# Feed-forward chunks 1 to 8 of a decoder layer: gate and up products computed together in eight PSUM banks, with two of eight pairs of K-blocks as seven products of sums

## The chip, the cores and the metric

The kernel runs on one core of a Trainium2 chip. The metric is the device time of one execution in microseconds (us). Of the kernel before there are three timed runs and one profiled execution.

## What is computed

One layer of a decoder trunk for 256 tokens of width 2048, in float32: a token mixer (retention, differential attention and a spatial gating unit, fed by one input projection and followed by an output projection) and a SwiGLU feed-forward of width 5632, each between two RMS norms. The part that matters here is the feed-forward:

```
h = rms_norm(x, pre_ffn_g[l])
f = (jax.nn.silu(h @ w_gate[l]) * (h @ w_up[l])) @ w_down[l]
x = x + rms_norm(f, post_ffn_g[l])
```

`h` is 256 x 2048, `w_gate` and `w_up` are 2048 x 5632, `w_down` is 5632 x 2048.

## The kernel before

Every large product is made of float32 operands that are split in two: `hi` is the operand rounded to the narrower matmul format fp32r (a ScalarE copy), `lo` is what is left (a VectorE subtraction). A product is then three matmuls, hi times hi, lo times hi, and hi times lo. The weights arrive as 512 KB pieces of two K-blocks (2 x 128 rows) by 512 columns; `split_weights` loads a piece into `raw` (4 buffers), writes `hi` (5 buffers) and `lo` (5 buffers). The activations, here `x1_hi` and `x1_lo`, stay in SBUF, transposed, with 256 tokens as two blocks `tb` of 128.

The hidden width of 5632 is walked in 11 chunks of 512 columns. For one chunk `matmul_chunk` runs over the eight weight pieces (16 K-blocks) of `w_gate` and accumulates one PSUM bank for each token block (the pool `acc`, 4 banks), then does the same for `w_up`. So a piece feeds 2 K-blocks x 2 token blocks x 3 = 12 matmuls of 128x512, and a chunk has 16 pieces, or 192 matmuls. `gate_part` reads the gate banks (tanh on ScalarE, then a VectorE operation) into a tile `fa`; `up_part` multiplies the up banks into it, waits one step, and then transposes the result: eight 128x128 transposes on TensorE into two tiles `h_ps` (the pool `tr`, 2 banks), a ScalarE copy to the hi half of the hidden activation and a VectorE subtraction to its lo half (line 582). The steps of `up_part` are taken by `advance()`, which is called after each weight piece.

The down projection already uses another scheme, in `seven_products`. Two token blocks and two K-blocks of the activation, and two K-blocks and two column chunks of the weights, are 2 x 2 blocks each; their product is formed with seven block products of sums instead of eight plain ones. The sums of the weight blocks are formed on VectorE from two raw pieces, the sums of the activation blocks once by `token_sums`. Seven banks collect the seven products over all pairs that use the scheme ("S" pairs); `partial_sums` then combines banks 0, 4, 5 and 6. Plain pairs ("P") add to banks 1, 2, 3 and 7, so that after both kinds each of the four results is one of these banks plus one partial sum. In the down projection one of three pairs is S. This stage uses all 8 banks; the pools are `acc` (4 banks), `tr` (2) and `mx` (2).

Instructions are written in program order; a scheduler then orders them for each engine and gives out the buffers of the pools, and an engine runs its own list strictly in that order. Loads are issued on SP's queue, in order.

Of the kernel before, what the change touches and what calls it, by code (L numbers as in the profile page):

```python
# [8 lines left out]
F32 = mybir.dt.float32  # L9
# [24 lines left out]
def trunk(  # L34
# [521 lines left out]
    h_parts = []  # L556
    for i, n in enumerate((2, 2, 2, 2, 3)):
        part = hpool.tile([P, 2, 4 * n, T], F32R, tag=f"h{i}", name=f"h{i}")
        h_parts += [(part, 4 * j) for j in range(n)]

    def h_chunk(c):
        part, k0 = h_parts[c]
        return part[:, 0, k0:k0 + 4], part[:, 1, k0:k0 + 4]

    def h_of(kb):
        hi, lo = h_chunk(kb // 4)
        return hi[:, kb % 4], lo[:, kb % 4]

    def up_part(c, aa, accs):
        for tb in range(NT):  # L570
            a = aa[tb]
            nc.vector.scalar_tensor_tensor(out=a, in0=a, scalar=hrr[:, tb:tb + 1], in1=accs[tb],
                                           op0=ALU.mult, op1=ALU.mult)
        yield
        for tb in range(NT):
            pt = ps_tr.tile([P, 4, P], F32, tag="tr", name="h_ps")
            for i in range(4):
                nc.tensor.transpose(out=pt[:, i], in_=aa[tb][:, i * P:(i + 1) * P], identity=ident)  # L578
            ts = slice(tb * P, (tb + 1) * P)
            h_hi, h_lo = h_chunk(c)  # L580
            nc.scalar.copy(out=h_hi[:, :, ts], in_=pt)
            nc.vector.tensor_tensor(out=h_lo[:, :, ts], in0=pt, in1=h_hi[:, :, ts].bitcast(F32), op=ALU.subtract)  # L582

    pending.append(up_part(0, aa, up0))
    for c in range(1, NCH):
        accs = matmul_chunk(w_gate[c], KB, 512, x1_of)
        aa = [gate_part(tb, accs[tb]) for tb in range(NT)]
        accs = matmul_chunk(w_up[c], KB, 512, x1_of)
        pending.append(up_part(c, aa, accs))


    actx.close()
    dn = ctx.enter_context(tc.tile_pool(name="dn", bufs=1))
    ss_f = const.tile([P, NT, 4], F32, tag="ss_f", name="ss_f")
    ss_t = const.tile([P, NT], F32, tag="ss_t", name="ss_t")
    ro_f = const.tile([P, NT], F32, tag="ro_f", name="ro_f")
    part_ss = const.tile([P, NT], F32, tag="part_ss", name="part_ss")
# [3 lines left out]
    def token_sums(c):  # L601

        hi, lo = h_chunk(c)
        tmp = dn.tile([P, 2, 1024], F32, tag="wide", name="sums_f")
        a = tmp[:, 0].rearrange("p (q e t) -> p q e t", q=2, e=2)
        f = tmp[:, 1].rearrange("p (q s t) -> p q s t", q=2, s=4)
        nc.vector.tensor_tensor(out=tmp[:, 0].rearrange("p (k t) -> p k t", k=4), in0=hi.bitcast(F32),
# [8 lines left out]
        home = dn.tile([P, 2, 2, 4, P], F32R, tag=f"sums{c}", name=f"sums{c}")  # L616
# [5 lines left out]
        for q in range(2):  # L622
            sums[2 * c + q] = [(home[:, 0, q, j], home[:, 1, q, j]) for j in range(4)]

    def fetch(n, p):
        raw = wraw.tile([P, 2, 512], F32, tag="raw", name="raw")
        nc.sync.dma_start(out=raw, in_=w_down[n][p])
        return raw
# [16 lines left out]
    def seven_products(n0, p):
        ra, rb = fetch(n0, p), fetch(n0 + 1, p)
        h1 = wsplit.tile([P, 2, 512], F32R, tag="hi", name="hi")
        l1 = wsplit.tile([P, 2, 512], F32R, tag="lo", name="lo")
        h22 = dn.tile([P, 512], F32R, tag="h22", name="hi_22")
        l22 = dn.tile([P, 512], F32R, tag="l22", name="lo_22")  # L650
# [4 lines left out]
        for out, in0, in1, op in ((ra[:, 0], ra[:, 0], rb[:, 0], ALU.subtract), (rb[:, 0], rb[:, 1], rb[:, 0], ALU.subtract),  # L655
# [11 lines left out]
        s1n, s2, s3, s4 = sums[p]  # L667
        return [[(0, h_block(2 * p, 0), (h1[:, 0], l1[:, 0])),
                 (1, h_block(2 * p + 1, 0), (h1[:, 1], l1[:, 1])),
# [4 lines left out]
                 (3, h_block(2 * p + 1, 1), (h2[:, 1], l2[:, 1]))]]  # L674

    def bank_tile(i):
        pool, tag = ((ps_tr, "tr"), (ps_acc, "acc"), (ps_acc, "acc"), (ps_acc, "acc"), (ps_tr, "tr"), (ps_mx, "mx"),
                     (ps_mx, "mx"), (ps_acc, "acc"))[i]
        return pool.tile([P, 512], F32, tag=tag, name=f"bank{i}")

    def down_columns(n0, new_fg, seq, extra, finish, tail_pairs, order):
# [4 lines left out]
        banks = {}  # L686
        kinds = [k for k, _ in seq]
        last_s = max(i for i, k in enumerate(kinds) if k == "S")
        left = {}
        for i, (k, _) in enumerate(seq):  # L690
            for b, n in (((1, 2), (2, 2), (3, 2), (7, 2)) if k == "P" else tuple((b, 1) for b in range(7))):
                left[b] = left.get(b, 0) + n
        for b, n in ((1, 2), (2, 2), (3, 2), (7, 2)):
            left[b] += n * len(tail_pairs)
        begun = set()

        def product(b, a, w):
            if b not in banks:
                banks[b] = bank_tile(b)
            left[b] -= 1  # L700
            (a_hi, a_lo), (w_hi, w_lo) = a, w
            nc.tensor.matmul(banks[b], lhsT=a_hi, rhs=w_hi, start=b not in begun, stop=False)  # L702
            nc.tensor.matmul(banks[b], lhsT=a_lo, rhs=w_hi, start=False, stop=False)  # L703
            nc.tensor.matmul(banks[b], lhsT=a_hi, rhs=w_lo, start=False, stop=left[b] == 0)  # L704
            begun.add(b)

        part = {}

        def partial_sums():
            u = dn.tile([P, 512], F32, tag="u", name="u")  # L710
            nc.scalar.copy(out=fg[:, 0, 0:512], in_=banks[0])
            nc.vector.tensor_tensor(out=u, in0=fg[:, 0, 0:512], in1=banks[5], op=ALU.add)
            nc.vector.tensor_tensor(out=fg[:, 0, 512:1024], in0=u, in1=banks[4], op=ALU.add)
            nc.vector.tensor_tensor(out=fg[:, 1, 512:1024], in0=fg[:, 0, 512:1024], in1=banks[6], op=ALU.add)
            nc.vector.tensor_tensor(out=fg[:, 1, 0:512], in0=u, in1=banks[6], op=ALU.add)

        for i, (k, p) in enumerate(seq):
            if i in extra:
                extra[i]()
            for part in (plain_pair(n0, p) if k == "P" else seven_products(n0, p)):  # L720
                for b, a, w in part:
                    product(b, a, w)
            advance()
            if i == last_s:
                fg = new_fg()
                partial_sums()
        parts = [plain_pair(n0, p) for p in tail_pairs]
# [28 lines left out]
    def new_fg(pool, tag):  # L756
# [5 lines left out]
                 {0: lambda: token_sums(2), 5: lambda: token_sums(3), 11: lambda: token_sums(4)}, close_chunk, [20, 21],  # L762
# [126 lines left out]
```

## Time and profile before

| | |
|---|---|
| median of 3 runs | 1139.25 us (1138.71 to 1139.56) |
| profiled execution, its own time | 1139.24 us |
| its span, first to last instruction | 1137.5 us |
| TensorE (PE) busy | 1123.8 us, 99% |
| VectorE (DVE) busy | 707.3 us, 62% |
| ScalarE (ACT) busy | 550.7 us, 48% |
| mean granted TensorE clock | 0.998 |

The busy time of TensorE overlaps itself, because the record of a matmul lasts longer than the distance to the next. What a matmul costs is read from the distance between starts. The feed-forward up to the last hidden chunk runs from about 400 us to 905 us, the down projection from about 894 us to the end.

### The profile page before, as it was taken

The numbers are of one execution on the slowest core, as the hardware profiler recorded it, in microseconds if no ns is written. First come the engines' busy times: TensorE is split into PE (matmuls) and PEld (weight loads), VectorE is DVE, ScalarE is ACT, GpSimd is POOL, SyncE is SP. The second block draws the span as 40 slices with busy tenths as digits, with TensorE's granted clock in tenths as the row PEclk, the third lists the DMA queues.
The fourth block names the chain that finished last, engine by engine and source line by source line (L and its number), as shares of the span: only waits on it lengthen the run. The fifth ranks groups of instructions, "written<-read, shape, count | busy, mean of one in ns | idle before, by whom it ended". The sixth has DMA issues, their size and how long they took to land.

```text
span 1137.5 us, 14030 instructions
## 1 busy us (share of the span) xinstructions
PE 1123.8 (99%) x5246; PEld 945.2 (83%) x5246; DVE 707.3 (62%) x867; ACT 550.7 (48%) x750; POOL 27.3 (2%) x55
## 2 busy tenths in 40 slices
PE   9999999999999999999999999999999999999996
PEld 7888899998888878888888888888888878888885
DVE  6655555656768596555554555555555787877775
ACT  7644455655644464444444444444444444555451
POOL 0000000000200000000000000000000000000000
PEclk9999999999999999999999999999999999999999
DMA  9755455565566446555555555555555366565662
GB/s 360 265 186 189 162 159 181 167 227 185 172 231 210 168 153 231 186 185 193 190 190 188 188 198 185 186 194 190 189 187 189 131 216 222 206 208 197 222 207 90
DMA packets 65013, 221.35 MB, mean 195 GB/s; under 512 B 7344, under 2 KB 9392, under 8 KB 64432
## 3 DMA queue, kind: packets, MB, share of 16 engines
q1 hardware_dynamic: 64656, 220.30, 57.1%
q8 instruction: 41, 0.67, 0.2%
q14 instruction: 28, 0.23, 0.1%
q10 hardware_dynamic: 288, 0.15, 0.1%
HBM read 218.32 MB, written 2.10 MB: 194 GB/s over the span
## 4 chain that ended last, share of the span: by engine, by line
PE 97%; DVE 1%; issue 1%; DMA 0%; ACT 0%; SPq 0%; POOLq 0%; POOL 0%; DVEq 0%; ACTq 0%
PE acc L90 25%; PE acc L88 25%; PE acc L89 25%; PE bank L704 6%; PE bank L703 6%; PE bank L702 6%; PE h_ps L578 1%; DMA raw<-in_w_ret_dram 0%; PE qk_ps L235 0%; PE sc L267 0%; PE x_ps L496 0%; PE yt_ps L191 0%; PE o_ps L244 0%; PE o_ps L243 0%; PE o_ps L242 0%
## 5 line engine op out<-in xcount | busy, mean ns | idle before, releaser
L81 DVE TENSOR_TENSOR lo<-raw,hi 128x1024 fp32r<-128x1024 f32 (+2 forms) x385 | 455.9, 1188 | 367.2 <-ACT hi L79 346.2
L79 ACT CAST hi<-raw 128x1024 fp32r<-128x1024 f32 (+2 forms) x385 | 391.3, 1019 | 456.2 <-PE acc L89 353.9
L88 PE MATMUL acc<-hi,x_hi 128*128 128x512 f32 (+1 forms) x1152 | 444.0, 385 | 1.2 <-ACT hi L79 0.7
L90 PE MATMUL acc<-lo,x_hi 128*128 128x512 f32 (+1 forms) x1152 | 438.3, 381 | 0.1
L89 PE MATMUL acc<-hi,x_lo 128*128 128x512 f32 (+1 forms) x1152 | 438.0, 380 | 0.0
L88 PEld LDWEIGHTS acc<-hi,x_hi 128*128 128x128 f32 x1152 | 216.5, 188 | 39.9 <-issue 2.0
L90 PEld LDWEIGHTS acc<-lo,x_hi 128*128 128x128 f32 x1152 | 216.2, 188 | 38.7 <-DVE lo L81 0.8
L89 PEld LDWEIGHTS acc<-hi,x_lo 128*128 128x128 f32 x1152 | 216.5, 188 | 36.6 <-DVE x_lo L184 0.2
L702 PE MATMUL bank<-hi,h 128*128 128x512 f32 x280 | 109.1, 390 | 0.0
L703 PE MATMUL bank<-hi,h 128*128 128x512 f32 x280 | 108.9, 389 | 0.0
L704 PE MATMUL bank<-lo,h 128*128 128x512 f32 x280 | 108.9, 389 | 0.0
L702 PEld LDWEIGHTS bank<-hi,h 128*128 128x128 f32 x280 | 52.6, 188 | 11.2 <-DVE h L582 0.4
L703 PEld LDWEIGHTS bank<-hi,h 128*128 128x128 f32 x280 | 52.6, 188 | 10.9
L704 PEld LDWEIGHTS bank<-lo,h 128*128 128x128 f32 x280 | 52.6, 188 | 10.8
L88 PE MATMUL acc<-hi,y_hi 128*128 128x512 f32 x128 | 50.3, 395 | 0.0
L89 PE MATMUL acc<-hi,y_lo 128*128 128x512 f32 x128 | 49.9, 391 | 0.0
L90 PE MATMUL acc<-lo,y_hi 128*128 128x512 f32 x128 | 49.8, 390 | 0.0
L662 ACT CAST hi_sb<-raw 128x1024 fp32r<-128x1024 f32 x12 | 12.6, 1050 | 39.9 <-DVE raw L657 37.0
L90 PEld LDWEIGHTS acc<-lo,y_hi 128*128 128x128 f32 x128 | 24.0, 188 | 5.0
L88 PEld LDWEIGHTS acc<-hi,y_hi 128*128 128x128 f32 x128 | 24.0, 188 | 5.1 <-ACT y_hi L193 0.3
L89 PEld LDWEIGHTS acc<-hi,y_lo 128*128 128x128 f32 x128 | 24.1, 188 | 4.9
L631 DVE TENSOR_TENSOR lo<-raw,hi 128x1024 fp32r<-128x1024 f32 (+1 forms) x24 | 22.4, 955 | 5.0 <-ACT hi L652 2.5
(183 smaller groups left out, 674.5 us busy)
## 6 DMA issues: line engine op xcount, KB each, us to landing
raw<-in_w_gate_dram SPq DMA_DIRECT2D x88, 512.0 KB, 3.5
raw<-in_w_up_dram SPq DMA_DIRECT2D x88, 512.0 KB, 3.5
raw<-in_w_down_dram SPq DMA_DIRECT2D x88, 512.0 KB, 4.5
raw<-in_w_ret_dram SPq DMA_DIRECT2D x47, 512.0 KB, 4.2
raw<-in_w_diff_dram SPq DMA_DIRECT2D x48, 384.0 KB, 3.1
raw<-in_w_out_dram SPq DMA_DIRECT2D x32, 512.0 KB, 4.2
raw<-in_w_sgu_dram SPq DMA_DIRECT2D x16, 512.0 KB, 3.9
x_sb<-in_x_dram SPq DMA_DIRECT2D x2, 1024.0 KB, 8.0
```

The costliest lines, as they stand in the source:

```text
L79: nc.scalar.copy(out=hi, in_=raw)
L81: nc.vector.tensor_tensor(out=lo, in0=raw, in1=hi.bitcast(F32), op=ALU.subtract)
L88: nc.tensor.matmul(ps, lhsT=a_hi, rhs=wh, start=first, stop=False)
L89: nc.tensor.matmul(ps, lhsT=a_lo, rhs=wh, start=False, stop=False)
L90: nc.tensor.matmul(ps, lhsT=a_hi, rhs=wl, start=False, stop=last)
L578: nc.tensor.transpose(out=pt[:, i], in_=aa[tb][:, i * P:(i + 1) * P], identity=ident)
L631: nc.vector.tensor_tensor(out=lo, in0=raw, in1=hi.bitcast(F32), op=ALU.subtract)
L662: nc.scalar.copy(out=h3, in_=rb)
L702: nc.tensor.matmul(banks[b], lhsT=a_hi, rhs=w_hi, start=b not in begun, stop=False)
L703: nc.tensor.matmul(banks[b], lhsT=a_lo, rhs=w_hi, start=False, stop=False)
L704: nc.tensor.matmul(banks[b], lhsT=a_hi, rhs=w_lo, start=False, stop=left[b] == 0)
```

## The change

For chunks 1 to 8 of the hidden width, gate and up are computed in one walk over the eight pairs of K-blocks (`gate_up`). Gate columns and up columns take the place of the two column chunks of the down projection, so that the scheme of seven products can be used: pairs 2 and 5 are S pairs, the other six are plain. An S pair has 7 x 3 = 21 matmuls where two plain pieces have 24. Chunks 0, 9 and 10 stay as they were, and so does the down projection, whose helpers are only made general.

All eight banks are in use. In an odd chunk the four plain banks (1, 2, 3, 7) lie in `acc` and the four shared ones (0, 4, 5, 6) in `mx` and `tr`; in an even chunk it is the other way round. After pair 5 `partial_sums` combines the shared banks into an SBUF tile `comb`; at the end of a chunk the plain banks are added to it, and tanh and the products follow from SBUF. The transposed hidden rows `h_ps` of a chunk go to banks of its own plain pool during the next chunk, which has its shared banks there. The sums of the activation blocks of pairs 2 and 5 are formed once, in `x1_sums`. The hidden activation is kept in more, smaller tiles, and the last ones serve as scratch (`m22`, `comb`, `sums_f`) until they are needed.

```
+    S_PAIRS = (2, 5)
+
+    def x1_sums(p):
+        tmp = hpool.tile([P, 2, 512], F32, tag="h10", name="sums_f")
+        home = gu.tile([P, 2, 1, 4, P], F32R, tag=f"sums{p}", name=f"sums{p}")
+        token_sums(("x1", p), 1, x1_hi[:, 2 * p:2 * p + 2], x1_lo[:, 2 * p:2 * p + 2], tmp, home)
+
+    def gate_up(c, extra):
+        odd = c % 2
+        plain = ("acc",) * 4 if odd else ("tr", "mx", "tr", "mx")
+        shared = ("mx", "tr", "tr", "mx") if odd else ("acc",) * 4
+        tags = dict(zip((1, 2, 3, 7, 0, 4, 5, 6), plain + shared))
+        kinds = ["S" if p in S_PAIRS else "P" for p in range(KB // 2)]
+        banks, product = products_into(kinds, bank_in(tags))
+        srcs = (w_gate[c], w_up[c])
+        comb = None
+        for p, k in enumerate(kinds):
+            if p in extra:
+                extra[p]()
+            if k == "P":
+                parts = plain_pair(srcs, p, x1_of)
+            else:
+                m22 = hpool.tile([P, 2, 512], F32R, tag="h9", name="m22")
+                parts = seven_products(srcs, p, x1_of, sums[("x1", p), 0], m22[:, 0], m22[:, 1])
+            for part in parts:
+                for b, a, w in part:
+                    product(b, a, w)
+            advance()
+            if p == S_PAIRS[-1]:
+                comb = hpool.tile([P, 4, 512], F32, tag="h10", name="comb")
+                partial_sums(banks, *(comb[:, i] for i in range(4)))
+        aa = []
+        for tb in range(NT):
+            g = comb[:, 2 * tb]
+            nc.vector.tensor_tensor(out=g, in0=g, in1=banks[(1, 3)[tb]], op=ALU.add)
+            a = ft.tile([P, 512], F32, tag="fa", name="fa")
+            nc.scalar.activation(out=a, in_=g, func=AF.Tanh, scale=hr2[:, tb:tb + 1])
+            nc.vector.scalar_tensor_tensor(out=a, in0=a, scalar=1.0, in1=g, op0=ALU.add, op1=ALU.mult)
+            aa.append(a)
+        for tb in range(NT):
+            u = comb[:, 2 * tb + 1]
+            nc.vector.tensor_tensor(out=u, in0=u, in1=banks[(2, 7)[tb]], op=ALU.add)
+        up_times(aa, [comb[:, 1], comb[:, 3]])
+        pending.append(later_rows(c, aa, "acc" if odd else "tr"))
+
     pending.append(up_part(0, aa, up0))
-    for c in range(1, NCH):
+    for c in range(1, 9):
+        gate_up(c, {0: lambda: x1_sums(2), 3: lambda: x1_sums(5)} if c == 1 else {})
+    for c in range(9, NCH):
         accs = matmul_chunk(w_gate[c], KB, 512, x1_of)
         aa = [gate_part(tb, accs[tb]) for tb in range(NT)]
         accs = matmul_chunk(w_up[c], KB, 512, x1_of)
```

The helpers of the S pairs are those of the down projection before, with the weights, the activation and the scratch as arguments; `partial_sums` and the weight sums are unchanged in their operations. In the changed file the subtraction that writes a lo half of weights in an S pair is line 605, the weight sums are lines 629 and 635, the additions of the plain banks lines 743 and 750, the product of gate and up line 695, and the lo half of the hidden rows line 691.

The instruction lists of the engines change at two places. The first is VectorE where one chunk ends and the next begins. Before, between the up products of a chunk (line 572) and its hidden rows (line 582), VectorE has three lo halves of the next chunk's weights:

```order
L81 TENSOR_TENSOR lo<-raw,hi 128x1024 x7
L572 SCALAR_TENSOR_TENSOR fa<-fa,hrr,acc 128x512 x2
L81 TENSOR_TENSOR lo<-raw,hi 128x1024 x3
L582 TENSOR_TENSOR h_4124<-h_ps,h_4124 128x4x128 x2
L81 TENSOR_TENSOR lo<-raw,hi 128x1024 x5
```

Now, at the turn from chunk 2 to chunk 3, it has this; the bank numbers are those of the plain banks 2 and 7:

```order
L746 SCALAR_TENSOR_TENSOR fa<-fa,comb 128x512 x2
L750 TENSOR_TENSOR comb<-comb,bank_4517 128x512
L750 TENSOR_TENSOR comb<-comb,bank_4521 128x512
L695 SCALAR_TENSOR_TENSOR fa<-fa,hrr,comb 128x512 x2
L605 TENSOR_TENSOR lo<-raw,hi 128x1024
L605 TENSOR_TENSOR m_4926<-raw,m_4926 128x512
L629 TENSOR_TENSOR raw<-raw 128x512 x3
L635 TENSOR_TENSOR raw<-raw 128x512
L605 TENSOR_TENSOR lo_sb<-raw,hi_sb 128x1024
L605 TENSOR_TENSOR lo_sa<-raw,hi_sa 128x1024
L81 TENSOR_TENSOR lo<-raw,hi 128x1024 x2
L691 TENSOR_TENSOR h_4916<-h_ps,h_4916 128x4x128 x2
```

All weight sums of the next chunk's first S pair, and the two lo halves of the pair behind it, have moved in between the end of a chunk and its hidden rows.

The second place is TensorE at the start of that S pair. Before, the eight transposes of the hidden rows stand between two plain pieces:

```order
L90 MATMUL acc<-lo,x_hi 128x512
L578 MATMUL h_ps<-ident,fa 128x128 x8
L88 MATMUL acc<-hi,x_hi 128x512
L89 MATMUL acc<-hi,x_lo 128x512
L90 MATMUL acc<-lo,x_hi 128x512
```

Now the S pair 2 of chunk 3 follows them; after the products of banks 0, 1, 2 and 6 (bank_4959 is bank 6) it opens bank 5 (bank_4963):

```order
L687 MATMUL h_ps<-ident,fa 128x128 x8
L664 MATMUL bank_4949<-hi,x_hi 128x512
...
L664 MATMUL bank_4861<-m_4926,sums_4127 128x512
...
L664 MATMUL bank_4959<-hi_sb,sums_4127 128x512
L665 MATMUL bank_4959<-hi_sb,sums_4127 128x512
L666 MATMUL bank_4959<-lo_sb,sums_4127 128x512
L664 MATMUL bank_4963<-hi_sb,sums_4127 128x512
```

Bank 5 and, after it, bank 4 take the two banks in which `h_ps` lay, so TensorE's first product there now stands behind VectorE's line 691. In the whole program TensorE's list goes from 4970 to 4922 rows.

## Rows read from the trace of the kernel before

**Rows 1.** The page: engines' busy time; granted TensorE clock in 40 slices.

```profile
PE 1123.8 (99%) x5246; PEld 945.2 (83%) x5246; DVE 707.3 (62%) x867; ACT 550.7 (48%) x750; POOL 27.3 (2%) x55
PEclk9999999999999999999999999999999999999999
```

**Rows 2.** The page: the chain that ended last, by engine and by line.

```profile
PE 97%; DVE 1%; issue 1%; DMA 0%; ACT 0%; SPq 0%; POOLq 0%; POOL 0%; DVEq 0%; ACTq 0%
PE acc L90 25%; PE acc L88 25%; PE acc L89 25%; PE bank L704 6%; PE bank L703 6%; PE bank L702 6%; PE h_ps L578 1%; DMA raw<-in_w_ret_dram 0%; PE qk_ps L235 0%; PE sc L267 0%; PE x_ps L496 0%; PE yt_ps L191 0%; PE o_ps L244 0%; PE o_ps L243 0%; PE o_ps L242 0%
```

**Rows 3.** The chain in order of time, 440 to 900 us: start, length, piece.

```profile
455.43 0.87 PE h_ps L578 x8
...
855.29 0.87 PE h_ps L578 x8
```

**Rows 4.** Stretches: length, busy of PE, PEld, DVE, ACT, POOL; clock, DMA, GB/s.

```profile
455.43:499.85 44.42, 44.42 (x202) 36.87 (x201) 23.48 (x22) 19.04 (x21) 0.00 (x0) 1.00 0.54 190
...
925.00:1080.00 155.00, 154.97 (x684) 128.37 (x685) 121.77 (x129) 80.52 (x89) 0.00 (x0) 1.00 0.64 214
```

**Rows 5.** VectorE's groups by shape: total, mean ns of one, idle before.

```profile
L81 DVE TENSOR_TENSOR lo<-raw,hi 128x1024 fp32r<-128x1024 f32 x335 | 408.6, 1224 | 325.2 <-ACT hi L79 308.1 <-PE h_ps L578 14.9
...
L657 DVE TENSOR_TENSOR raw<-raw 128x512 f32<-128x512 f32 x36 | 24.8, 689 | 0.7
L572 DVE SCALAR_TENSOR_TENSOR fa<-fa,hrr,acc 128x512 f32<-128x512 f32 x22 | 16.2, 744 | 0.0
L541 DVE SCALAR_TENSOR_TENSOR fa<-fa,acc 128x512 f32<-128x512 f32 x22 | 15.0, 684 | 0.9 <-ACT fa L540 0.8
...
L582 DVE TENSOR_TENSOR h<-h_ps,h 128x512 fp32r<-128x512 f32 x22 | 14.1, 683 | 0.0
```

**Rows 6.** VectorE in order of time, one S pair of the down projection: start, length, operation.

```profile
964.02 1.82 DVE L631 TENSOR_TENSOR lo<-raw,hi 128x1024 fp32r<-128x1024 f32 x2 [0.94 <-ACT hi L651]
965.76 2.14 DVE L657 TENSOR_TENSOR raw<-raw 128x512 f32<-128x512 f32 x3
...
969.09 1.23 DVE L631 TENSOR_TENSOR lo_sb<-raw,hi_sb 128x1024 fp32r<-128x1024 f32 x1 [0.47 <-ACT hi_sb L662]
970.23 1.22 DVE L631 TENSOR_TENSOR lo_sa<-raw,hi_sa 128x1024 fp32r<-128x1024 f32 x1
971.37 2.35 DVE L81 TENSOR_TENSOR lo<-raw,hi 128x1024 fp32r<-128x1024 f32 x2
```

**Rows 7.** VectorE in order of time, partial sums of the down projection.

```profile
994.49 0.68 DVE L715 TENSOR_TENSOR fg<-u,bank 128x512 f32<-128x512 f32 x1
995.09 1.22 DVE L81 TENSOR_TENSOR lo<-raw,hi 128x1024 fp32r<-128x1024 f32 x1
```

**Rows 8.** All engines in order of time, a plain piece's turn in chunk 3.

```profile
550.43 1.05 ACT L79 CAST hi<-raw 128x1024 fp32r<-128x1024 f32 x1 [1.67 <-PE acc L89]
550.46 0.39 PE L88 MATMUL acc<-hi,x_hi 128*128 128x512 f32 x1
...
551.51 1.23 DVE L81 TENSOR_TENSOR lo<-raw,hi 128x1024 fp32r<-128x1024 f32 x1 [1.50 <-ACT hi L79]
```

**Rows 9.** VectorE, then TensorE's weight loads, at the down projection's first S pair.

```profile
907.98 1.28 DVE L582 TENSOR_TENSOR h<-h_ps,h 128x512 fp32r<-128x512 f32 x2
...
908.16 0.19 PEld L704 LDWEIGHTS bank<-lo_sb,sums 128*128 128x128 f32 x1
908.72 0.19 PEld L702 LDWEIGHTS bank<-hi,h 128*128 128x128 f32 x1 [0.36 <-DVE h L582]
```

**Rows 10.** DMA issues: line engine operation count, KB each, median us to landing.

```profile
raw<-in_w_up_dram SPq DMA_DIRECT2D x88, 512.0 KB, 3.5
raw<-in_w_down_dram SPq DMA_DIRECT2D x88, 512.0 KB, 4.5
```

**Rows 11.** Who waited for whom, 890 to 1135 us: total, times, longest.

```profile
ACT hi L79 <- DMA raw<-in_w_down_dram: 21.8, 13, 4.6
```

**Rows 12.** Stretch with the end of chunk 0; columns as in rows 4.

```profile
435.00:455.00 20.00, 20.00 (x90) 16.57 (x89) 10.75 (x10) 7.34 (x7) 0.00 (x0) 1.00 0.65 225
```

More of the change, by code (lines that the diff above doesn't have):

```diff
@@ L555, in trunk @@
     hpool = ctx.enter_context(tc.tile_pool(name="hpool", bufs=1, side="right"))
[L556 to L559, printed above, removed]
+    gctx = actx.enter_context(ExitStack())
+    gu = gctx.enter_context(tc.tile_pool(name="gu", bufs=1))
+    h_parts = {}
     def h_chunk(c):
+        if c not in h_parts:
+            n = 2 if c < 8 else 1
+            part = hpool.tile([P, 2, 4 * n, T], F32R, tag=f"h{c}", name=f"h{c}")
+            for j in range(n):
+                h_parts[c + j] = (part, 4 * j)
         part, k0 = h_parts[c]
@@ L567, in h_of, with token_sums @@
         return hi[:, kb % 4], lo[:, kb % 4]
[L569 to L584, printed above, removed]
-    for c in range(1, NCH):
[L586 to L597, printed above, removed]
     TB = (slice(0, P), slice(P, 2 * P))
     sums = {}
[L601 to L607, printed above, removed]
+    def token_sums(key, pairs, hi, lo, tmp, home):
+        n = pairs * 512
+        a = tmp[:, 0].rearrange("p (q e t) -> p q e t", q=pairs, e=2)
+        f = tmp[:, 1].rearrange("p (q s t) -> p q s t", q=pairs, s=4)
+        nc.vector.tensor_tensor(out=tmp[:, 0].rearrange("p (k t) -> p k t", k=2 * pairs), in0=hi.bitcast(F32),
                                 in1=lo.bitcast(F32), op=ALU.add)
@@ L621, in token_sums, with fetch @@
         nc.vector.tensor_tensor(out=s_lo, in0=flat, in1=s_hi.bitcast(F32), op=ALU.subtract)
-        for q in range(2):
-            sums[2 * c + q] = [(home[:, 0, q, j], home[:, 1, q, j]) for j in range(4)]
-    def fetch(n, p):
+        for q in range(pairs):
+            sums[key, q] = [(home[:, 0, q, j], home[:, 1, q, j]) for j in range(4)]
+    def fetch(piece):
         raw = wraw.tile([P, 2, 512], F32, tag="raw", name="raw")
-        nc.sync.dma_start(out=raw, in_=w_down[n][p])
+        nc.sync.dma_start(out=raw, in_=piece)
         return raw
@@ new lines, in products_into, with product @@
+    def products_into(kinds, new_bank):
+        left = {}
+        for k in kinds:
+            for b, n in (PLAIN if k == "P" else tuple((b, 1) for b in range(7))):
+                left[b] = left.get(b, 0) + n
+        banks = {}
+        def product(b, a, w):
+            start = b not in banks
+            if start:
+                banks[b] = new_bank(b)
+            left[b] -= 1
+            (a_hi, a_lo), (w_hi, w_lo) = a, w
+            nc.tensor.matmul(banks[b], lhsT=a_hi, rhs=w_hi, start=start, stop=False)
+            nc.tensor.matmul(banks[b], lhsT=a_lo, rhs=w_hi, start=False, stop=False)
+            nc.tensor.matmul(banks[b], lhsT=a_hi, rhs=w_lo, start=False, stop=left[b] == 0)
+        return banks, product
@@ new lines, in hidden_rows @@
+    def hidden_rows(c, aa, tag):
+        for tb in range(NT):
+            pt = POOL_OF[tag].tile([P, 4, P], F32, tag=tag, name="h_ps")
+            for i in range(4):
+                nc.tensor.transpose(out=pt[:, i], in_=aa[tb][:, i * P:(i + 1) * P], identity=ident)
+            ts = slice(tb * P, (tb + 1) * P)
+            h_hi, h_lo = h_chunk(c)
+            nc.scalar.copy(out=h_hi[:, :, ts], in_=pt)
+            nc.vector.tensor_tensor(out=h_lo[:, :, ts], in0=pt, in1=h_hi[:, :, ts].bitcast(F32), op=ALU.subtract)
@@ L685, in down_columns @@
             load_in_order(gp[j], post_ffn[(n0 + j) * 512:(n0 + j + 1) * 512].partition_broadcast(P))
-        banks = {}
         kinds = [k for k, _ in seq]
         last_s = max(i for i, k in enumerate(kinds) if k == "S")
[L689 to L715, printed above, removed]
+        banks, product = products_into(kinds + ["P"] * len(tail_pairs), bank_in(dict(enumerate(
+            ("tr", "acc", "acc", "acc", "tr", "mx", "mx", "acc")))))
+        srcs = (w_down[n0], w_down[n0 + 1])
         for i, (k, p) in enumerate(seq):
```

83 lines of the change are left out of this document (60 added, 23 removed).

## The prediction

> **What bounds the kernel now.** I read the page first, then the chain of waits, then one chunk of the stage that changes. TensorE is busy 99% of the span, at full granted clock in every slice [rows 1]. The chain that ended last is TensorE for 97%, and its pieces are matmuls, one after the other [rows 2]. So the kernel is as long as its matmuls are, and an edit pays what it takes off TensorE's list, as long as the other engines stay ahead.
>
> The price of one matmul comes from the chain in order of time. The eight transposes of hidden rows come once a chunk; from 455.43 to 855.29 us there are ten such groups, nine periods, so a chunk takes 399.86 / 9 = 44.43 us [rows 3]. The transposes take 0.87 of it, the 192 matmuls of 128x512 the rest: (44.43 - 0.87) / 192 = **0.2269 us** each. In that chunk TensorE never stops, and VectorE is busy 23.48 of 44.42 us, ScalarE 19.04 [rows 4]. The down projection, which mixes S pairs and plain pairs already, keeps TensorE busy for 154.97 of 155.00 us while VectorE is busy for 121.77, or 79% [rows 4].
>
> **What is removed.** Eight chunks with two S pairs each lose 3 matmuls a pair: 48, which is also the fall of TensorE's list from 4970 to 4922 rows. 48 x 0.2269 = **10.89 us**, 1.36 a chunk. A chunk becomes 44.43 - 1.36 = 43.07 us.
>
> **What is added to VectorE.** A plain pair costs it two lo halves of 1.224 us; an S pair three lo halves, one half-size lo and four weight sums, 3 x 1.22 + 5 x 0.69 = 7.1 us [rows 5, 6]. A chunk has 12 x 1.224 = 14.7 for plain pairs, 14.2 for the two S pairs, and 14 operations of 512 columns (four partial sums, four additions of plain banks, four for tanh and product, two hidden-row halves) at about 0.69, 9.7 together. The sum is 38.6 us of 43.07, 90%, where it was 53% before. ScalarE goes to about 23 of 43 us by the same count (its copies are 1.05 us [rows 8]). So VectorE stays under TensorE on average, but its list is in strict order, and the question is whether one wait of TensorE falls on a late place of it.
>
> **The new wait.** It is bank 5 in S pair 2 of chunks 1 to 8. That bank is free only when VectorE has read the hidden rows (line 691, 582 before), and this read stands behind the whole S split and two more lo halves. Behind TensorE's waiting instruction stands everything else. I count from E, the end of a chunk's last matmul.
>
> TensorE asks for bank 5 after two plain pairs (48 matmuls, 10.89), the transposes (0.87) and four products (12 matmuls, 2.72): at E + 14.48.
>
> VectorE's side, with starts from rows. The last weight piece before E is split when the gate piece of pair 7 gives its buffer back, 12 matmuls or 2.72 us before E. In the trace ScalarE starts 0.03 before such a turn and VectorE 1.08 after ScalarE [rows 8], so this lo half starts at E - 1.67. Lo halves of 1024 columns start 1.14 apart (969.09 to 970.23 to 971.37 [rows 6]); operations of 512 columns 0.60 apart (994.49 to 995.09 [rows 7]). From the first weight sum to `lo_sb` there are 3.33 us (965.76 to 969.09 [rows 6]), the ScalarE copy between them included. The list then gives:
> - lo half to E - 0.53; two operations behind tanh and two up additions, 4 x 0.60, to E + 1.87; the two products at their full 0.744 [rows 5], to E + 3.36
> - lo half 1.14, half-size lo 0.60, to E + 5.10; weight sums 3.33, to E + 8.43
> - `lo_sb`, `lo_sa`, first lo half of pair 3, 3 x 1.14, to E + 11.85. The second lo half needs a buffer that TensorE gives back at E + 10.89, so it can start at E + 10.86 + 1.08 = E + 11.94. That is 0.09 later and sets the time
> - 1.14 more, then the hidden rows for 0.68 [rows 5]: done at E + 13.76.
>
> TensorE's request comes **0.72 us later**. The down projection has had this wait once: at 907.98 VectorE began the same two reads, the first was done 0.68 later, at 908.66, and the weight load that waited for it came at 908.72 [rows 9]. So 0.06 goes to the signal and 0.66 is left. I take this wait as 0 and keep the bounds: below, no gain from it; above, the rivals.
>
> **Other edits, taken at nothing.** The shared banks are read in pairs 6 and 7 and needed by the next chunk's plain products, some 8 us later; without that cover the four additions would cost 4 x 0.6 a chunk. The plain banks 2 and 7 are read by E + 1.87 and needed as banks 0 and 6 after E + 11.76. The sums of the activation are two sets of two operations of 512 and four of 128 columns, at most 2 x (2 x 0.69 + 4 x 0.69) = 8.3 us if a small one costs as much as a large one; the scheduler puts the first set into chunk 0, at whose end VectorE is idle for 20 - 10.75 = 9.25 us of 20 [rows 12]. The loads move the same bytes, but an S pair holds its two raw buffers until `lo_sa`: pair 4's loads can start only at E + 10.7. Landing takes 3.5 us, or 4.5 among S pairs [rows 10], a copy and a lo half 2.3 more: E + 17.5, and TensorE comes there at E + 11.76 + 45 x 0.2269 = E + 21.97. ScalarE did wait for loads among S pairs, 21.8 us in 13 times [rows 11], but TensorE was busy all the same [rows 4].
>
> **Sum.** The profiled execution took 1139.24 us, 1.74 more than its span, and 0.01 less than the median, 1139.25. 1139.24 - 10.89 = 1128.35: **1128.4 us**. About 0.2% (2.3 us) is what a measurement of this kernel can tell from no change; this is 0.95%.
>
> **Rivals.**
> - *VectorE's operations don't overlap.* Then the list goes by durations: from E - 1.67, 1.22 + 4 x 0.684 + 2 x 0.744 + 1.22 + 0.69 + 3.33 + 4 x 1.22 + 0.68 gives E + 14.57, plus 0.06: TensorE waits 0.15 at eight places, 1.2 us, **1129.6**. Against it: the second `lo` of a pair starts 1.14 after the first, though one lasts 1.22 [rows 6]. The Trainium skill, VectorE: DVE Perf Modes, section The DRAIN you can't avoid, says that the next operation does not start until the pipeline is empty after each one; these rows show starts 0.08 before the recorded end, so the trace does not bear it out as far as records tell. Chance 0.12.
> - *The mix is dearer than its parts*, because operations that read PSUM and SBUF in this order cost more than where I took them. The chain from E - 0.53 to E + 13.76 is 14.3 us; 5% more uses up the slack, 10% makes 1.43 - 0.66 = 0.77 at eight places, 6.2 us, **1134.5**; between the two, 1132. For it: at 90% VectorE has little to catch up with. Against it: the same operations took the same 0.68 to 0.69 wherever they stand. Chance 0.14.
> - *Slower: pair 3's weights land late*, and the hidden rows wait behind them on VectorE. Their buffer is free at E - 0.5, landing at E + 4.0, needed by ScalarE at E + 10.86: 6.9 us of cover. It decides against the change from 6.9 + 0.66 + 1.36 = 8.9 us of delay. The longest wait of ScalarE for a load among S pairs was 4.6 us [rows 11]. At 10 us late TensorE loses 2.4 at eight places: 1128.4 + 19.5 = **1147.9**. Chance 0.04.
> - *The change doesn't do what it says.* The list has exactly 48 matmuls less, so only a dearer matmul could take it back; the same alternation of banks in the down projection shows 684 records in 155.00 us, or 0.2266 [rows 4]. Chance 0.02.
>
> **How the numbers follow.** The forecast has 0.68, with a range of its own of 1127.4 to 1129.3 (runs before lay 0.85 apart). The range for 8 in 10 goes from 1127.0 to 1133.0: it takes in the first rival and the milder half of the second, and leaves out the rest. Faster 0.94 (all but the last two rivals), same 0.02, slower 0.04.
>
> **What would show it.** Right: hidden-row transposes 43.07 us apart in chunks 1 to 8; 48 records of 128x512 fewer; VectorE near 38 us busy a chunk; no idle time of TensorE behind line 691. Wrong: idle time at line 664 on bank 5, put down to line 691, eight times of equal length; a period over 43.3; TensorE idle for `lo_sb` in pair 5; or a longer distance of matmuls.

## The result and the profile after

| | before | after |
|---|---|---|
| median | 1139.4 us (4 runs, 1138.71 to 1139.98) | **1127.91 us** (4 runs, 1127.62 to 1128.06) |
| ratio | | 0.9899, 95% interval 0.9882 to 0.9916 |
| profiled execution | 1139.24 us | 1127.93 us |

The change makes the kernel faster by 11.5 us; 10.9 were forecast. The page after, its row of busy time and its chain by engine, answers to [rows 1, 2]:

```profile
PE 1113.6 (99%) x5198; PEld 937.4 (83%) x5198; DVE 817.0 (73%) x1039; ACT 578.4 (51%) x792; POOL 27.5 (2%) x55
...
PE 96%; DVE 2%; DMA 1%; issue 1%; ACT 0%; POOL 0%; POOLq 0%; DVEq 0%; ACTq 0%; SPq 0%
```

TensorE still sets the end. The count of its records fell from 5246 to 5198, by the 48 matmuls. The chain in order of time has the hidden-row transposes of eight chunks (start, length, piece; answers to [rows 3]):

```profile
461.05 0.87 PE h_ps L687 x8
...
762.52 0.87 PE h_ps L687 x8
```

There are seven periods between them: (762.52 - 461.05) / 7 = 43.07 us, where it was 44.43. One such period as a stretch (columns as in [rows 4]):

```profile
504.10:547.19 43.09, 43.09 (x197) 35.74 (x195) 36.66 (x43) 22.32 (x26) 0.00 (x0) 1.00 0.61 196
```

TensorE doesn't stop in it, and VectorE is busy for 36.66 us, 85%. Last, all engines in order of time where TensorE opens bank 5 in chunk 2 (VectorE's reads of the hidden rows, the weight load (PEld) of that product, the product):

```profile
505.03 1.23 DVE L81 TENSOR_TENSOR lo<-raw,hi 128x1024 fp32r<-128x1024 f32 x1 [0.21 <-ACT hi L79]
...
506.18 1.28 DVE L691 TENSOR_TENSOR h<-h_ps,h 128x512 fp32r<-128x512 f32 x2
...
507.36 0.19 PEld L664 LDWEIGHTS bank<-hi_sb,sums 128*128 128x128 f32 x1
...
507.58 0.39 PE L664 MATMUL bank<-hi_sb,sums 128*128 128x512 f32 x1
```

The first read takes 0.68 us and is over at 506.86; the product starts 0.72 us later. Neither the weight load nor the product has a wait, and from the end of the read to the start of the load there are 0.50 us.

### The profile page after: what moved, and what is told of

Its sections match the earlier page's. It is cut to its first block, busy times and chain, and to the rows that moved or that the text cites. A ratio compares the mean times of both kernels' runs of the same rounds, so it can differ in the third digit from the quotient of the medians.

```text
span 1126.2 us, 14203 instructions
## 1 busy us (share of the span) xinstructions
PE 1113.6 (99%) x5198; PEld 937.4 (83%) x5198; DVE 817.0 (73%) x1039; ACT 578.4 (51%) x792; POOL 27.5 (2%) x55
## 4 chain that ended last, share of the span: by engine, by line
PE 96%; DVE 2%; DMA 1%; issue 1%; ACT 0%; POOL 0%; POOLq 0%; DVEq 0%; ACTq 0%; SPq 0%
PE bank L666 16%; PE bank L664 16%; PE bank L665 16%; PE acc L88 15%; PE acc L90 14%; PE acc L89 14%; PE h_ps L687 1%; DMA raw<-in_w_down_dram 1%; PE qk_ps L235 0%; PE sc L267 0%; DMA cols<-in_cols_dram 0%; PE yt_ps L191 0%; DVE x_lo L499 0%; DVE lo L81 0%; PE o_ps L243 0%
## 5 line engine op out<-in xcount | busy, mean ns | idle before, releaser
L88 PE MATMUL acc<-hi,x_hi 128*128 128x512 f32 (+1 forms) x640 | 244.5, 382 | 0.7 <-ACT x_hi L183 0.7
L89 PE MATMUL acc<-hi,x_lo 128*128 128x512 f32 (+1 forms) x640 | 239.5, 374 | 0.0
L90 PE MATMUL acc<-lo,x_hi 128*128 128x512 f32 (+1 forms) x640 | 239.2, 375 | 0.0
L664 PE MATMUL bank<-hi,x_hi 128*128 128x512 f32 x416 | 162.5, 391 | 0.0
L666 PE MATMUL bank<-lo,x_hi 128*128 128x512 f32 x416 | 161.9, 389 | 0.0
L665 PE MATMUL bank<-hi,x_lo 128*128 128x512 f32 x416 | 161.8, 389 | 0.0
L88 PEld LDWEIGHTS acc<-hi,x_hi 128*128 128x128 f32 x640 | 120.6, 188 | 19.5 <-issue 2.0
L90 PEld LDWEIGHTS acc<-lo,x_hi 128*128 128x128 f32 x640 | 120.5, 188 | 18.3
L89 PEld LDWEIGHTS acc<-hi,x_lo 128*128 128x128 f32 x640 | 120.7, 189 | 17.0 <-DVE x_lo L184 0.2
L666 PEld LDWEIGHTS bank<-lo,x_hi 128*128 128x128 f32 x416 | 78.1, 188 | 16.3
L664 PEld LDWEIGHTS bank<-hi,h 128*128 128x128 f32 x280 | 52.6, 188 | 11.1 <-DVE h L691 0.4
L666 PEld LDWEIGHTS bank<-lo,h 128*128 128x128 f32 x280 | 52.6, 188 | 10.9
L665 PEld LDWEIGHTS bank<-hi,h 128*128 128x128 f32 x280 | 52.6, 188 | 10.9
```

The costliest lines, as they stand in the source:

```text
L88: nc.tensor.matmul(ps, lhsT=a_hi, rhs=wh, start=first, stop=False)
L89: nc.tensor.matmul(ps, lhsT=a_lo, rhs=wh, start=False, stop=False)
L90: nc.tensor.matmul(ps, lhsT=a_hi, rhs=wl, start=False, stop=last)
L664: nc.tensor.matmul(banks[b], lhsT=a_hi, rhs=w_hi, start=start, stop=False)
```

## The experiments

All times below are medians beside runs of the kernel before on the same chip, which lay between 1138.9 and 1139.5 us. "The changed kernel" is the one at 1127.9; the kernel before was 1139.4 beside it, so a difference from it of less than about 0.5 us says nothing.

**1. The same banks without the seven products.**

```diff
-    S_PAIRS = (2, 5)
+    S_PAIRS = ()
...
-            g = comb[:, 2 * tb]
-            nc.vector.tensor_tensor(out=g, in0=g, in1=banks[(1, 3)[tb]], op=ALU.add)
+            g = banks[(1, 3)[tb]]
...
-        up_times(aa, [comb[:, 1], comb[:, 3]])
+        up_times(aa, [banks[2], banks[7]])
```

> The change with no pair of K-blocks as seven products: chunks 1 to 8 still take gate and up together in eight banks whose roles swap, every pair plain, no token sums, no partial sums; the work computed is the reference's. Theory (only the number of matmuls pays): the 48 matmuls are back, 1127.9 + 48 x 0.2269 = 1138.8 us, hidden-row transposes 43.07 + 6 x 0.2269 = 44.43 us apart, the time before within 0.2%. Rival (the layout of banks itself pays, by a wait that it takes away): below 1137.

Measured: 1139.0 us, ratio to before 0.9998 (0.9990 to 1.0007). The chain in order of time:

```profile
461.20 0.87 PE h_ps L687 x8
...
772.20 0.87 PE h_ps L687 x8
```

The period is (772.20 - 461.20) / 7 = 44.43 us, as before. So taking gate and up together, swapping the banks' roles and splitting the tiles of the hidden activation are worth nothing by themselves. The gain is the 48 matmuls: 1139.0 - 1127.9 = 11.1 us, 0.231 each.

**2. One more instruction in front of bank 5.** The bank 5 slot is free when VectorE has read the hidden rows; here that read is made twice.

```diff
-            nc.vector.tensor_tensor(out=h_lo[:, :, ts], in0=pt, in1=h_hi[:, :, ts].bitcast(F32), op=ALU.subtract)
+            for _ in range(2 if tb == 0 and c < 8 else 1):
+                nc.vector.tensor_tensor(out=h_lo[:, :, ts], in0=pt, in1=h_hi[:, :, ts].bitcast(F32), op=ALU.subtract)
```

> The changed kernel in which VectorE subtracts the first half of the hidden rows twice instead of once, in chunks 0 to 7: one more instruction of 128x512, at the same place of VectorE's row, that keeps bank 5's slot 0.60 to 0.68 us longer. Theory (slack of 0.66 to 0.72 us at bank 5, nothing is lost inside it): within 0.1 us per chunk, 1127.9 to 1128.7. Rival (no slack left, each added VectorE microsecond ahead of bank 5 is paid): 8 x 0.64 = 5.1 us, 1133. Rival (VectorE's share of the period decides, 90% is not the limit): 1127.9 here as well; the next kernel parts it from the theory.

Measured: 1128.91 us (1128.50 to 1129.39), 1.0 us more than the changed kernel and just above the theory's range. In the stretch from 440 to 800 us the list of waits (total, times, longest) had no entry for TensorE or its weight loads; now it has one for the loads and still none for the matmuls:

```profile
PEld bank L664 <- DVE h L692: 1.6, 8, 0.2
```

The transposes are (763.06 - 460.93) / 7 = 43.16 us apart. The eight waits of 0.2 us are those of bank 5. An instruction that moves the release by 0.60 us (the distance between starts, [rows 7]) makes the weight load 0.19 us late, so the slack was about 0.41 us at the load, not 0.66. The rows of the changed kernel say nearly the same: 0.50 us from read to load, less 0.06 for the signal. The load runs ahead of its product, which takes up half of the delay: 0.09 us per chunk are lost, 0.7 of the 1.0 us.

**3. Three more instructions.** The same edit with 4 in the place of 2.

> The same instruction four times instead of once in chunks 0 to 7; by VectorE's row one 128x1024 subtraction also comes between, so bank 5's slot is let go 3 x 0.60 + 1.14 = 2.9 to 3 x 0.68 + 1.14 = 3.2 us later. Theory (the bank is the limit, slack 0.66): TensorE waits 2.3 to 2.5 us at the opening of bank 5, eight times: 1127.9 + 18 to 20 = 1146 to 1148 us, transposes 45.3 to 45.6 us apart. Rival (VectorE's load is the limit): 38.6 + 1.9 = 40.5 us of VectorE in a chunk, still under 43.07, so 1127.9. Rival (the wait is made up later in the chunk): between the two.

Measured: 1130.9 us (1128.95 to 1132.78, a wider spread than any other kernel here). Theory and first rival both miss, and the number falls where the second rival had it. But nothing is made up later in the chunk. All engines in order of time, at the place shown above:

```profile
505.97 1.88 DVE L692 TENSOR_TENSOR h<-h_ps,h 128x512 fp32r<-128x512 f32 x3
...
507.31 0.19 PEld L664 LDWEIGHTS bank<-hi_sb,sums 128*128 128x128 f32 x1 [0.19 <-DVE h L692]
...
511.32 0.68 DVE L692 TENSOR_TENSOR h<-h_ps,h 128x512 fp32r<-128x512 f32 x1
...
512.05 0.50 PE L664 MATMUL bank<-hi_sa,sums 128*128 128x512 f32 x1 [0.35 <-DVE h L692]
```

I had read only VectorE's row of this kernel. The scheduler had set TensorE's anew too: bank 5 takes the slot that VectorE lets go with its second read, and the product for bank 4, which gets the slot held to 512.00, stands behind twelve matmuls of pair 3. So the delay became a wait of 0.35 us, in this one chunk; in all eight the load for bank 5 waits 0.2 us, as in experiment 2. The profiled execution is the fastest of the five, 1128.95 us: what made the others up to 3.8 us longer is not shown. To price the wait itself, the order has to be held.

**4. The same, with TensorE in the order of the program.**

```diff
-            nc.tensor.matmul(banks[b], lhsT=a_hi, rhs=w_hi, start=start, stop=False)
+            first = nc.tensor.matmul(banks[b], lhsT=a_hi, rhs=w_hi, start=start, stop=False)
+            if pin:
+                tc.keep_in_program_order(first)
...
-                    product(b, a, w)
+                    product(b, a, w, pin=p in (2, 3))
```

> The kernel with the instruction four times, and TensorE's products of pairs 2 and 3 held in the order of the program. In the run without that, the order on TensorE had changed: the banks' slots went to the products in the order in which VectorE was to free them, bank 4's products stood behind twelve of pair 3, and its weight load still waited 0.78 us for VectorE's last instruction, at 512.05; the products with bank 5 waited 0.19 us. Theory (the slot held by the repeated instruction stops everything behind it on TensorE): in the program's order the same slot is asked for at about 508.0 and is free at 512.0, so 4.0 us are lost in each of eight chunks: 1128.3 + 32 = 1160 us, transposes 47.1 us apart. Rival (the slot is not what TensorE waits for, or the chunk makes the wait up): as the run without it, 1129 to 1133.

Measured: 1171.2 us (1169.67 to 1172.87), 43 us more than the changed kernel. TensorE's waits from 440 to 840 us:

```profile
PE bank L664 <- DVE h L694: 28.0, 8, 4.6
```

Eight waits, 3.5 us on the mean (six of 3.2, one of 4.2, one of 4.6), behind the line that the theory named: the direction is the theory's, and the rival falls. The product that waits opens bank 4, which has the slot of the repeated reads here too. The size is 11 us above it. Stretches around one wait (clock is the number before the last two):

```profile
505.00:512.80 7.80, 7.80 (x40) 6.38 (x38) 7.12 (x9) 5.96 (x7) 0.00 (x0) 1.00 0.54 160
512.80:516.36 3.56, 0.36 (x3) 0.03 (x1) 3.41 (x4) 1.44 (x2) 0.00 (x0) 1.00 0.90 322
516.36:518.50 2.14, 2.14 (x6) 1.66 (x7) 0.69 (x1) 0.23 (x1) 0.00 (x0) 0.54 0.82 247
518.50:520.50 2.00, 2.00 (x7) 1.62 (x6) 0.71 (x1) 1.04 (x1) 0.00 (x0) 0.64 0.31 119
520.50:522.50 2.00, 2.00 (x10) 1.61 (x10) 1.90 (x4) 0.00 (x0) 0.00 (x0) 1.00 0.00 0
```

After 3.2 us without work TensorE runs at a granted clock of 0.54 for 2.14 us and of 0.64 for 2.00 us, near the lower level of 1.2 GHz, and then at 2.4 GHz again. That costs 2.14 x 0.46 + 2.00 x 0.36 = 1.7 us more. All eight waits are followed by it: the same sum gives 1.7 us behind each of the six short ones and 2.8 and 2.6 behind the two long ones, 15.6 us together. With the 28.0 us of waiting that makes 43.6; the median is 43.3 us above the changed kernel, the profiled execution 44.9.

**5. The three more instructions, and the seven products one pair later.** Experiment 3's edit, with pairs 3 and 6 in place of 2 and 5.

```diff
-    S_PAIRS = (2, 5)
+    S_PAIRS = (3, 6)
```

> The kernel with the instruction four times, and the seven products on pairs 3 and 6 instead of 2 and 5: the same VectorE work per chunk, but TensorE opens bank 5 one plain pair, 24 x 0.2269 = 5.4 us, later. Theory (the bank's deadline is the limit): the wait of 2.3 to 2.5 us is covered, 1127.9 us within 0.2%, transposes 43.07 us apart. Rival (VectorE's load is the limit): as slow as the kernel with pairs 2 and 5, about 1147.

Measured: 1128.0 us (1127.94 to 1128.44), and TensorE waits for nothing between 440 and 800 us. The period is the one of the changed kernel, (762.59 - 461.11) / 7 = 43.07:

```profile
461.11 0.87 PE h_ps L687 x8
...
762.59 0.87 PE h_ps L687 x8
```

VectorE has as many instructions as in experiments 3 and 4, and they cost nothing here. The scheduler set the lists anew, so the place of both sides has to be read again. VectorE's last read of `h_ps`, and TensorE's first product for bank 4, in chunk 2 (each engine in order of time):

```profile
510.99 0.68 DVE L692 TENSOR_TENSOR h<-h_ps,h 128x512 fp32r<-128x512 f32 x1
```

```profile
513.77 0.39 PE L664 MATMUL bank<-hi_sa,sums 128*128 128x512 f32 x1
```

From the first transpose (504.01 here, 508.64 in experiment 4) the last read is over after 7.7 us, in experiment 4 after 7.6. TensorE asks for the bank after 9.8 us, in experiment 4 after 4.4. So the release stayed where it was and the request moved. It is not the amount of work on VectorE that decides, but the place at which TensorE asks for a bank.

**6. Three pairs as seven products.**

```diff
-    S_PAIRS = (2, 5)
+    S_PAIRS = (2, 4, 6)
```

with the sums of the third pair in memory of the later hidden rows.

> The changed kernel with three pairs of K-blocks as seven products (2, 4 and 6) in chunks 1 to 8; the same output. If only the matmuls counted: 24 fewer, 1127.9 - 24 x 0.2269 = 1122.5 us. Theory (VectorE is the next bound): a pair of seven products costs VectorE 0.60 + 4 x 0.60 + 3 x 1.14 = 6.4 us in place of 2 x 1.14, so 38.6 + 4.1 = 42.7 us in a chunk whose matmuls need 41.7; with its own waits of about 0.5 us a pair it can't keep up: transposes 42.7 to 44.5 us apart instead of 43.07, 1125 to 1139 us, and TensorE waits for lo, lo_sb or a bank behind VectorE.

Measured: 1156.2 us (1155.68 to 1160.30), ratio to before 1.0158 (1.0144 to 1.0173). The direction is the theory's, the size far beyond its range. (The 41.7 us of matmuls in the text is my slip: three pairs leave 183 matmuls and the transposes, 42.39 us. The texts of experiments 7 and 8 have it too.) TensorE's waits from 440 to 800 us, and the sum over seven stretches from 461 to 790 us:

```profile
PE bank L666 <- DVE lo L81: 4.2, 4, 1.9
PE bank L666 <- DVE lo_sb L605: 3.2, 8, 0.5
PE bank L664 <- DVE h L691: 2.9, 2, 2.4
PE h_ps L687 <- DVE fa L695: 2.8, 2, 2.3
PE bank L664 <- ACT hi_sb L634: 1.3, 3, 0.7
```

```profile
sum 329.00, PE 314.50 PEld 251.92 DVE 287.54 ACT 166.82 POOL 0.00; mean PE 44.93 PEld 35.99 DVE 41.08 ACT 23.83 POOL 0.00
```

All but 1.3 us of TensorE's waits are behind VectorE, 14.4 us in all. The matmuls behind a wait come late too (behind a stop of 2.4 us the granted clock was 0.51 from 511.09 to 514.43): added up from 440 to 840 us, the distances between their starts are 33 us over 0.2269 each, which is the whole loss. Yet VectorE is busy for only 287.54 of 329.00 us, 87%. Half of its idle time (20 of about 41 us, by its groups) stands before lo halves in the pairs of seven products, whose hi halves ScalarE has not copied yet. ScalarE's waits for loads in the same stretch, and the waits of SP's queue before it issues them:

```profile
ACT hi L623 <- DMA raw<-in_w_gate_dram: 28.0, 14, 4.3
ACT h_early L624 <- DMA raw<-in_w_up_dram: 26.9, 18, 4.1
```

```profile
SPq L601 <- DVE lo_sb L605: 82.1, 14, 7.0
SPq L77 <- DVE lo L81: 66.4, 57, 7.0
SPq L601 <- DVE lo L81: 51.1, 14, 8.3
```

A pair of seven products holds two of the four raw buffers until VectorE's last half, and the next loads start only then. SP's queue waits as much in the changed kernel (115.8 us behind `lo_sb`, 9.5 at longest), where it costs nothing; what is new is that ScalarE waits for the loads, 54.9 us where the same two lines waited 4.6. VectorE's work and the ring of buffers hang together: a late VectorE frees buffers late, and late weights hold up VectorE. The two following kernels try to part VectorE's work from this ring.

**7. Three pairs, with two instructions of each pair on GpSimd.**

```diff
-        lo_of(l22, rb[:, 1], h22)
+        side.tensor_tensor(out=l22, in0=rb[:, 1], in1=h22.bitcast(F32), op=ALU.subtract)
...
-        nc.vector.tensor_tensor(out=ra[:, 1], in0=ra[:, 1], in1=rb[:, 1], op=ALU.subtract)
+        side.tensor_tensor(out=ra[:, 1], in0=ra[:, 1], in1=rb[:, 1], op=ALU.subtract)
```

> The kernel with three pairs as seven products (1156.2 us), in chunks 1 to 8 with two of VectorE's 128x512 instructions of each such pair (the low half of the second row's weights, the last of the four sums of weights) on GpSimd; the same output. Theory (VectorE's work per chunk is what made it slow): VectorE has 3 x 2 x 0.60 = 3.6 us less in a chunk, 42.7 - 3.6 = 39.1 us against matmuls of 41.7: back to 1122.5 us if nothing else waits, at most 1130. Rival (the chain of one pair, weights to sums to halves, is what comes late, and GpSimd lengthens it; no row of this kernel shows a 128x512 operation on GpSimd, so its price is open): 1156 or more.

Measured: 1164.5 us (1162.60 to 1166.19), slower still, as the rival said. Groups by shape (total, mean ns of one, idle before), GpSimd's two and one of VectorE's from 450 to 800 us:

```profile
L626 POOL TENSOR_TENSOR h_early<-raw,h_early 128x512 fp32r<-128x512 f32 x24 | 32.7, 1363 | 257.3 <-ACT h_early L624 249.4 <-PE bank L666 7.9
L635 POOL TENSOR_TENSOR raw<-raw 128x512 f32<-128x512 f32 x24 | 31.1, 1296 | 69.8 <-DVE raw L629 69.8
...
L629 DVE TENSOR_TENSOR raw<-raw 128x512 f32<-128x512 f32 x66 | 60.1, 911 | 6.4 <-DMA raw<-in_w_up_dram 2.3 <-DVE raw L629 0.5
```

What VectorE does in 0.69 us takes GpSimd 1.30 to 1.36, and VectorE's own weight sums (line 629) beside it grow from 690 to 911 ns. The Trainium skill, SBUF — State Buffer, section SBUF: two separate sides, says that a VectorE operation with two SBUF inputs and GpSimd share a pair of ports which one holds for a whole instruction while the other waits. The trace agrees in direction: three weight sums take 2.22 us where no GpSimd instruction runs beside them (from 502.19) and 3.18 where one does (from 512.91). How much of the time lost comes from this, and how much from the longer chain that the rival named, is not parted.

**8. Three pairs, with those two instructions left out.**

```diff
-        lo_of(l22, rb[:, 1], h22)
+        l22 = h22
...
-        nc.vector.tensor_tensor(out=ra[:, 1], in0=ra[:, 1], in1=rb[:, 1], op=ALU.subtract)
```

> The kernel with three pairs as seven products (1156.2 us), and two of VectorE's 128x512 instructions of each such pair left out in chunks 1 to 8: the low half of the second row's weights (its high half is multiplied in its place, so the matmuls stay as many) and the last of the four sums of weights. This takes out of VectorE's row what the run on GpSimd moved, without that run's dearer instructions. Theory (VectorE's work per chunk is what made three pairs slow): 42.7 - 3.6 = 39.1 us of VectorE against 41.7 of matmuls, 1122.5 to 1130 us. Rival (the six raw buffers that three pairs hold, of four, and the order at the chunk's end limit, whatever VectorE's sum): 1145 us or more.

Measured: 1136.9 us (1135.49 to 1140.65): 19 of the 34 us above 1122.5 are gone, 14 are left. It falls between the two theories. The first chunks reach the period of 42.39 us that the matmuls alone give, (545.76 - 460.98) / 2; then the waits begin, almost all of them in one place:

```profile
PE bank L668 <- DVE h L695: 9.7, 6, 2.4
```

That is bank 5 again, and it is the largest wait that remains. Taking two of VectorE's instructions out of each pair gives back more than half of what three pairs cost. It doesn't show that the work alone did it: the shorter chain also frees the raw buffers earlier, and ScalarE's waits for the loads of these pairs fell from 54.9 to 35.3 us. How much is the ring of raw buffers stays open, since no run here has a fifth buffer.

**9. Nine joint chunks, ten, and each with more time at the start of the down projection.** Nine: the loop runs to chunk 9 with the banks' roles begun the other way round. Ten: it runs to chunk 10, whose `m22` takes the memory of the last hidden rows.

```diff
-    for c in range(1, 9):
+    for c in range(1, 11):
...
-    down_columns(0, lambda: new_fg(dn, "wide"), sequence(pattern, range(4, 10), [0, 1, 2, 3] + list(range(10, 20))),
+    down_columns(0, lambda: new_fg(dn, "wide"), sequence("P" + pattern[:-1], range(4, 10), [0, 1, 2, 3] + list(range(10, 20))),
```

The second line is the shift, one more plain pair ahead of the first seven products; it is in the last two kernels only.

> The changed kernel with chunk 9 done jointly too, the roles of the banks begun the other way round (chunk 0's hidden rows then go to the banks of acc, so that the plain chunk 10 finds its own free); the same output. Theory (only the number of matmuls pays): 6 fewer, 1127.9 - 1.36 = 1126.6 us. Rival (the start of the joint chunks or of chunk 10 waits for a bank in the new roles): 1127.9 or above.

> The changed kernel with chunks 9 and 10 done jointly too (chunk 10's second-row weights lie in the memory of the last hidden rows); the same output. If only the matmuls counted: 12 fewer, 1127.9 - 2.72 = 1125.2 us. Theory: VectorE now closes chunk 10's gate and up (about 2.4 us more than a plain chunk leaves) right ahead of the sums of the hidden rows, for which the down projection's first seven products already wait: up to 2.4 us of it come back there, 1125.2 to 1127.6 us.

> The kernel with chunks 1 to 9 done jointly, with the same shift of the down projection's first six pairs of products; the same output. The run with nine gave 1127.05 us, its profiled execution 0.2 us of TensorE idle on lo_sb at the start of the down projection and 0.6 us of waiting weight loads. Theory: that returns, 1126.2 to 1126.9 us. Rival (nothing waits long enough there): 1127.05.

> The kernel with chunks 1 to 10 done jointly, and in the first half of the down projection one more plain pair ahead of the first seven products (each of the six pairs one place later); the same output. The run with ten joint chunks gave 1126.75 us where 12 fewer matmuls alone would have given 1125.2: TensorE waited for lo_sb behind VectorE's sums at the start of the down projection. Theory (that is where the 1.5 us are): 5.4 us more time for VectorE there brings them back, 1125.2 to 1125.8 us. Rival (they are lost elsewhere): 1126.75 as before.

| | without the shift | with it | fewer matmuls alone |
|---|---|---|---|
| nine | 1127.05 us (1126.60 to 1127.21) | 1126.13 us (1125.98 to 1126.29) | 1126.6 us |
| ten | 1126.75 us (1125.94 to 1126.97) | **1124.62 us** (1124.50 to 1125.25) | 1125.2 us |

Nine falls between its theory and its rival, ten inside its range; with the shift both come out a little below their ranges. TensorE's wait in the down projection of the ten without the shift:

```profile
PE bank L666 <- DVE lo_sb L605: 0.5, 1, 0.5
```

With the shift that entry is gone. The best kernel is ten chunks with the shift: 1124.62 us, 0.9877 of before (0.9863 to 0.9890) and 3.3 us under the changed kernel. For ten the shift gave 2.1 us, more than the 1.5 that I looked for and than the wait of 0.5. Matmuls that come late without an idle TensorE make up most of the difference: from 860 to 1118 us the distances between starts hold 1.8 us more without the shift than with it, 0.7 us for nine. The changed kernel itself has 0.6 us of that, which would explain why both kernels with the shift lie below the number that the matmuls alone give; the changed kernel with the shift and nothing else was not run. Steps this small are near what a measurement can tell, and the kernels with and without the shift ran on different chips.

## Why the prediction was right

- **The price of a matmul and the period.** 43.07 us was forecast and is what the chain shows. Experiment 1 gives the 48 matmuls back, and with them the whole gain.
- **VectorE's load** was put too high, at 38.6 us or 90%; it is 36.66 or 85%. I had added durations, while instructions start before the record of the last one ends. The first rival of experiment 3 (40.5 us) and the theory of experiment 6 (42.7) carry the same excess.
- **The new wait at bank 5.** The place was right: in experiment 2 it is the only thing that a weight load waits for, and in experiment 8 the first and largest wait of TensorE. From the start of the transposes at 504.10, E is 493.21; the read is over at E + 13.65 (13.76 in the forecast) and the product starts at E + 14.37 (14.48). The distance of 0.72 is exact. The term that is mis-sized is the slack left of it, 0.66 us: what waits is the weight load, which is issued ahead of the product, and about 0.41 us were left. The forecast didn't need the difference, but rival two did: it would begin to cost at about 3% (0.41 of 14.3 us) and not at 5%. That nothing was lost here was calculated, but with less to spare than the prediction says: one instruction of 0.60 us more and the load waits.
- **First rival, operations don't overlap:** no. Two reads of 683 ns take 1.28 us together. The Trainium skill, VectorE: DVE Perf Modes, section The DRAIN you can't avoid, says that the next operation does not start until the pipeline is empty, but also that one which is not held back starts earlier; the prediction took up only the first half. Here the next one starts 0.08 us before the recorded end of the last, as before the change, which agrees with the second half.
- **Second rival, the mix is dearer:** no. VectorE's groups after, by shape, answer to [rows 5]:

```profile
L81 DVE TENSOR_TENSOR lo<-raw,hi 128x1024 fp32r<-128x1024 f32 x303 | 368.5, 1223 | 191.9 <-ACT hi L79 186.1 <-PE bank L665 3.1 <-PE h_ps L687 1.5
...
L691 DVE TENSOR_TENSOR h<-h_ps,h 128x512 fp32r<-128x512 f32 x22 | 14.1, 683 | 0.0
L695 DVE SCALAR_TENSOR_TENSOR fa<-fa,hrr,comb 128x512 f32<-128x512 f32 x16 | 11.3, 749 | 0.0
```

- **Third rival, pair 3's weights land late:** no. ScalarE's longest wait for a load in these chunks was 2.0 us, and none reached TensorE.
- **The remaining 0.4 to 0.6 us.** The profiled executions differ by 11.31 us, 0.42 more than the sum; the medians by 0.6 more, which is well inside the interval of the ratio (about 2 us either way). In the profiled executions, the gain at the last transposes is 905.17 - 894.47 = 10.70; the rest comes in the down projection's second S pair, where TensorE waited before, and after only a weight load did. Before, TensorE's wait from 900 to 930 us:

```profile
PE bank L704 <- DVE lo_sb L631: 0.5, 1, 0.5
```

The VectorE instruction that was late there, before and after, from VectorE in order of time:

```profile
914.04 1.23 DVE L81 TENSOR_TENSOR lo<-raw,hi 128x1024 fp32r<-128x1024 f32 x1 [2.98 <-ACT hi L79]
```

```profile
902.82 1.22 DVE L81 TENSOR_TENSOR lo<-raw,hi 128x1024 fp32r<-128x1024 f32 x1 [2.45 <-ACT hi L79]
```

VectorE waits 0.53 us less for a piece of `w_down`, although its load is issued 1.36 us after the start of the last transposes in both (906.53 and 895.83). The profiled execution of experiment 1 has no such stall either, and took as long as before. So this looks like a load that landed later in one execution, and not like a term of the change that I had missed; with one profile of each kernel it isn't shown, and why the load was late stays open.

## What to carry to other kernels

When a change makes two engines share banks, don't compare their busy shares: count from one event, on both lists, to the place where one asks for what the other gives back, and take the weight load, not the matmul, as the one that asks. Moving that place is cheaper than saving work: one pair later covered three more instructions for nothing, while the same instructions cost 43 us where TensorE had to stand still in the program's order. And where a scheduler sets the order, an experiment that adds work must be read on every engine's list before it runs, since the order may move away from the very wait that it is to price.

## What was not expected of the hardware

- A stop of 3.2 us of TensorE was followed by 4.1 us at a granted clock of 0.54 to 0.64. Stops of 0.5 us, and one of 1.9 us in experiment 6, were not followed by anything (clock 1.00). Of two stops of 2.4 us in experiment 8, the one that ended at 596.68 was not either, and the one that ended at 686.68 was (0.52 from 687.58 to 690.91). A bank's wait can so cost half as much again as its length.
- A subtraction of 128x512 took 1.30 to 1.36 us on GpSimd and 0.69 on VectorE, and VectorE's weight sums in that kernel took a third longer on the mean.
- The weight load that runs ahead of its product hides half of a wait of 0.19 us: 0.09 us a chunk were paid. A list of TensorE's idle time doesn't show such losses; the distances between the starts of its matmuls do.
